# Compression and rotation ahead of the delta rule's matrices, in tiles of their own, with half-array products in pairs

## The chip, the core and the metric

The kernel runs on one core of one Trainium2 chip. The metric is the device time of one execution in microseconds. The engines are TensorE (PE, with its weight loads as PEld), VectorE (DVE), ScalarE (ACT), GpSimd (POOL) and SyncE (SP, which here only starts transfers).

## The reference, cut to what matters

A trunk of two layers over 256 tokens of width 1024. Each layer has a mixer with two branches, the gated delta rule (a) and attention (b), mixed by gates, and then a feed-forward part: dense in layer 0, eight experts in layer 1.

```python
for l in range(DEPTH):
    h = rms_norm(x, norm_mix[l]) * (1.0 + sc_m) + sh_m
    proj = h @ w_in[l]
    ...
    o_a = gated_delta_rule(d_q, d_k, d_v, beta, g_log)
    o_a = rms_norm(o_a, dn_norm[l]) * jax.nn.silu(dn_z.reshape(b_, s_, DN_HEADS, DN_DV))
    y_a = o_a.reshape(b_, s_, DN_HEADS * DN_DV) @ w_oa[l]
    n_q = apply_rope(rms_norm(n_q...), cos, sin)             # s_k and w_k likewise
    k_c = compress_blocks(c_k...)                            # then norm and rotation; v_c likewise
    o_b = nsa_core(n_q, k_c, v_c, s_k, s_v, w_k, w_v, gates) # compressed, selected, window
    y_b = o_b @ w_ob[l]
    gate_a, gate_b = jnp.split(jax.nn.sigmoid(m_g), 2, -1)
    x = x + g_m * ((gate_a * y_a + gate_b * y_b) @ w_out[l])
    h = rms_norm(x, norm_ffn[l]) * (1.0 + sc_f) + sh_f
    x = x + g_f * (swiglu(h, ...) if l % 2 == 0 else moe_ffn(h, ...))

# gated_delta_rule, chunks of 64 tokens: lower and a_intra are products over the head's
# 64 dimensions times a decay; tinv is the inverse of a unit lower triangle
lower = where(strict, einsum('nbhcd,nbhsd->nbhcs', kb, kc) * decay, 0)
tinv = triangular_solve(eye + lower, eye)
a_intra = where(tril, einsum('nbhcd,nbhsd->nbhcs', qc, kc) * decay, 0)
# compress_blocks: 15 windows of 32 tokens, 2 groups
blk = x[:, idx] + pos_emb                                    # 32 * 64 numbers a window
return silu(blk @ w1) @ w2
```

## The kernel before

Tokens lie in two tiles of 128. Large products are made in three parts from a high and a low piece of each operand (lines 242 to 244, or 373 to 375 for the tiles called pn). The pieces of a weight are made on ACT (line 236) and DVE (line 238), after SP's queue has brought it into a ring of slots: a slot is free again when DVE has made the low piece.

The order in which the program is written sets priorities, and a scheduler makes from it the fixed order of each engine: an instruction written later may fill a hole if its tiles are free. A tile with a tag takes its place in turn with the other tiles of that tag, so a later tile waits until the earlier one has had its last reader. PSUM has eight banks: three for "dn" (delta rule), two for "ns" (attention), two for "pj" (projections) and one more.

The mixer (line 435) is written in this order:

1. The projections of the delta rule's inputs (pj), the short convolution and norms, some projections of attention (pn, into npq and npk).
2. The delta rule's matrices. For four heads at a time: the keys times their write strength (kb, line 577), the decays on a pair of masks (pd, lines 588 to 596, exponentials E0 and E1), then for each head the products pS of keys with kb and with the queries (qk). Each pS has 64 dimensions in the contraction, thus half the array's rows. DVE multiplies it with the decay (line 604 for the 512 columns of the first token tile, 609 for the second).
3. The inverse, on blocks of 16: a chain of 15 steps of three DVE instructions (the tile UU, lines 622, 623, 624), which starts at line 618 and ends at line 637. Products of 32 and 64 (py, p, p2, lines 641 to 663) make it whole. Then the recurrence over chunks (pz, pw, pX, po, lines 674 to 696), and the norm of the result (of, to line 722).
4. Attention's compression (lines 726 to 784). Transposed windows (zbk) times the first weights give pcc, one branch (keys, values) after the other with 64 output columns, thus half the array's columns. After the activation (s1, s2) come the second weights (pkv), norm and rotation (kvc, kd), the transposed keys (pkc, kcT) and the values (pvb).
5. The other projections of attention, norm and rotation of queries and keys (rn, npq, npk, qr), and their transposes (pt, into qT and kT).
6. Attention: compressed() (psc), then the window and selected parts in eight groups: scores pSs, masked on DVE to pr, exponentials on ACT, transposes (ppt), products with the values (pob). The tile acc gathers them.
7. The mixing gates (function gates, line 926): 96 products for each 512 columns into pj, and Tanh on ACT (line 931) into a tile mg0 or mg1. Then the branch outputs, and the product with w_out.

In the order that the scheduler makes, much of 4 to 7 is laid between 2 and 3. The constants lie in one tile ct, 1290 columns wide; 406 of these are a pad, and from the masks on the tile is used again for the router's row of gate factors (gfr). The tile E0 shares its tag with qT, L32 with the attention's transposed weights pT, the masks with kT, and zbk with qs.

Layer 1's experts (function moe) take their weights from the same queue (line 1181). They begin at 915 us in the profiled execution.

Of the kernel before, what the change touches and what calls it, by code (L numbers as in the profile page):

```python
# [16 lines left out]
P = 128  # L17
# [23 lines left out]
def const_table():  # L41
# [34 lines left out]
    parts["pad"] = np.zeros((P, 406), np.float32)  # L76
# [11 lines left out]
def trunk(ctx, tc, A, out, dbg=None, stop=None):  # L88
# [39 lines left out]
    def bc(ap, shape):  # L128
        return ap.to_broadcast(shape)
# [257 lines left out]
    cs = cst.tile([P, 2, 3, 32], F32, name="cs")  # L387

# [46 lines left out]
    def mixer(l, hx, mp, late, begun=()):  # L435
# [87 lines left out]

        pq = bank("dn", "pq")
# [30 lines left out]
        masks = mq.tile([P, 2, P], F32R, tag="kT", name=f"masks{l}")  # L555
# [9 lines left out]
        L32 = T([P, 16, 32], "L32", 2, tag="pT")  # L565
# [3 lines left out]
        for hh, hs in enumerate(halves):  # L569
# [9 lines left out]
            E0 = T([P, 4, NT, P], "E0", tag="qT")  # L579
# [18 lines left out]
            for a in range(4):  # L598
                h_ = hh * 4 + a
                b, r = h_ // 2, slice((h_ % 2) * 64, (h_ % 2) * 64 + 64)  # L600
                pS = bank("dn", "pS")
                mm(pS[:, 0:S], kf[r, b, 0:P], kb[r, b], start=True, stop=True)
                mm(pS[:, S:2 * S], kf[r, b, 0:P], qf[r, b], start=True, stop=True)
                V.tensor_tensor(L0[hh][:, a], v2(pS), bc(E0[:, a, None].rearrange("p o t i -> p o (t i)"), [P, 2, S]),
                                op=OP.mult)
                pS = bank("dn", "pS")
                mm(pS[:, 0:P], kf[r, b, P:S], kb[r, b, P:S], start=True, stop=True)
                mm(pS[:, P:S], kf[r, b, P:S], qf[r, b, P:S], start=True, stop=True)
                V.tensor_tensor(L1[:, h_], v2(pS[:, 0:S]), bc(E1[:, a, None], [P, 2, P]), op=OP.mult)
# [113 lines left out]

        proj(npc, 0, 256)

        s1 = T([64, 2, 32], "s1")
        s2 = T([64, 2, 32], "s2")
        w2 = T([64, 2, 64], "w2c")
        nc.scalar.dma_start(w2, A["w_cmp2"][l].rearrange("k d e -> d k e"))
        for kv in range(2):  # L730
            zb = T([P, 16, 31], "zbk", tag="zb")
            pz = bank("ns", "pzc")
            for g in range(2):
                for t in range(NT):
                    tr(pz[:, g * S + t * P:g * S + t * P + P], npc[:, t, kv * 2 + g].rearrange("p a d -> p (a d)"))
# [864 lines left out]
```

## Time and profile before

| | |
|---|---|
| median of three runs | 1817.03 us (1811.85 to 1820.92) |
| the profiled execution | 1813.39 us, of which the span is 1811.6 us |
| mean granted clock of PE | 0.961 of full speed |

The page shows the busy time of each engine, the chain of work that ended last, and the costliest groups of instructions. A row of the timeline has the start in us, the length in us, the engine, the line, the operation, the tile written and the tiles read, the shape, and how many instructions it stands for; in square brackets is the idle time of the engine ahead of it, and what ended that. Matmuls are pipelined, so the step from one start to the next, not the length, says what one costs. A row of a group has the busy time, the mean length of one in ns, and the idle time ahead of them with what ended most of it.

### The profile page before, as it was taken

How to read it: one execution, taken by the hardware profiler on the slowest of the kernel's cores; microseconds unless marked ns; L12 is line 12 of the kernel's file. 1: busy time of each engine (PE TensorE's matmuls, PEld its weight loads, DVE VectorE, ACT ScalarE, POOL GpSimd, SP SyncE). 2: the span in 40 equal slices, each digit the busy share in tenths (PEclk: the TensorE clock that was granted, in tenths of full speed). 3: DMA queues.
4: the chain of work that ended last, by engine and by line, in shares of the span. 5: the costliest groups of instructions: out<-in, count | busy, mean ns of one | idle time of the engine just before them, and what ended most of it. 6: DMA issues, size and time to landing. Idle time of an engine off the chain costs nothing.

```text
span 1811.6 us, 29467 instructions
## 1 busy us (share of the span) xinstructions
PE 1736.5 (96%) x11324; PEld 1386.8 (77%) x11324; DVE 1271.8 (70%) x2146; ACT 935.2 (52%) x1372; POOL 61.4 (3%) x114
## 2 busy tenths in 40 slices
PE   6889799899999999999999999999999999999997
PEld 4879678899999898987888735788885367878732
DVE  6769757799995777834699713888984078999811
ACT  3664344444444574543477602777772067777600
POOL 4300000100000100000100000000000000000000
PEclk8899779999999899988999999999999999999999
DMA  9547325599984334413779999999999999999997
GB/s 336 162 141 255 119 72 190 205 345 329 329 278 151 125 111 135 157 47 140 266 271 367 328 397 404 409 403 409 377 363 360 403 409 407 405 399 362 345 392 277
DMA packets 206362, 515.38 MB, mean 284 GB/s; under 512 B 18862, under 2 KB 58358, under 8 KB 206214
## 3 DMA queue, kind: packets, MB, share of 16 engines
q1 hardware_dynamic: 196806, 509.45, 75.9%
q10 hardware_dynamic: 9312, 3.90, 0.8%
q8 instruction: 91, 1.49, 0.3%
q14 instruction: 57, 0.47, 0.1%
q0 software_dynamic: 96, 0.07, 0.0%
HBM read 512.34 MB, written 1.05 MB: 283 GB/s over the span
## 4 chain that ended last, share of the span: by engine, by line
PE 90%; DVE 5%; ACT 2%; issue 1%; DMA 1%; ACTq 0%; DVEq 0%
PE ph L1204 21%; PE py L1235 11%; PE ph L1267 8%; PE pj L242 8%; PE pj L244 7%; PE pj L243 7%; PE py L1294 4%; PE pSs L876 2%; PE pob L896 2%; PE py L244 2%; PE py L242 1%; PE py L243 1%; PE pn L373 1%; PE pn L375 1%; PE pn L374 1%
## 5 line engine op out<-in xcount | busy, mean ns | idle before, releaser
L238 DVE TENSOR_TENSOR wml<-m,wmh 128x1024 fp32r<-128x1024 f32 (+1 forms) x300 | 311.1, 1078 | 34.3 <-ACT wmh L236 31.4
L236 ACT ACTIVATE wmh<-m 128x1024 fp32r<-128x1024 f32 (+1 forms) x302 | 276.5, 945 | 64.1 <-PE ph L1204 36.8
L1204 PE MATMUL ph<-wml,gh 128*128 128x512 f32 x560 | 181.7, 397 | 2.0 <-DVE wml L238 2.0
L1204 PE MATMUL ph<-wmh,gl 128*128 128x512 f32 x560 | 181.9, 394 | 0.0
L1204 PE MATMUL ph<-wmh,gh 128*128 128x512 f32 x560 | 181.6, 394 | 0.2 <-ACT gh L1144 0.2
L236 ACT ACTIVATE w2h<-m 128x1024 fp32r<-128x1024 f32 x130 | 134.7, 1057 | 41.8 <-PE py L1235 28.3
L238 DVE TENSOR_TENSOR w2l<-m,w2h 128x1024 fp32r<-128x1024 f32 x130 | 152.6, 1220 | 5.1 <-ACT w2h L236 4.8
L1235 PE MATMUL py<-w2h,uu 128*128 128x512 f32 x560 | 152.8, 394 | 0.0
L1267 PE MATMUL ph<-m,gs 128*64 128x512 f32 (+1 forms) x720 | 139.7, 537 | 0.0
L1204 PEld LDWEIGHTS ph<-wml,gh 128*128 128x128 f32 x560 | 103.8, 188 | 32.1 <-DVE wml L238 7.3
L242 PE MATMUL pj<-hf0h,wh 128*128 128x256 f32 x448 | 127.1, 285 | 1.2 <-ACT hf0h L344 1.2
L243 PE MATMUL pj<-hf0l,wh 128*128 128x256 f32 x448 | 126.7, 284 | 0.0
L244 PE MATMUL pj<-hf0h,wl 128*128 128x256 f32 x448 | 126.5, 285 | 0.0
L1204 PEld LDWEIGHTS ph<-wmh,gh 128*128 128x128 f32 x560 | 105.0, 188 | 26.3 <-ACT wmh L236 1.6
L1235 PEld LDWEIGHTS py<-w2h,uu 128*128 128x128 f32 x560 | 105.1, 188 | 24.5
L1204 PEld LDWEIGHTS ph<-wmh,gl 128*128 128x128 f32 x560 | 105.1, 188 | 24.2
L263 DVE SCALAR_TENSOR_TENSOR adacc<-ada,cact,adacc 128x512 f32<-128x512 f32 x158 | 117.3, 757 | 2.5 <-DMA ada<-in_w_ada_dram 1.4
L1267 PEld LDWEIGHTS ph<-m,gs 128*64 128x64 f32 x720 | 51.3, 137 | 81.9 <-issue 74.0
L236 ACT ACTIVATE wh<-w 128x1024 fp32r<-128x1024 f32 x56 | 59.4, 1061 | 95.0 <-PE pj L243 60.5
L1277 DVE TENSOR_TENSOR u<-u,ph 128x512 f32<-128x512 f32 (+1 forms) x12 | 7.5, 622 | 135.8 <-PE ph L1267 135.8
L236 ACT ACTIVATE wh<-win 128x1024 fp32r<-128x1024 f32 x64 | 67.3, 1056 | 66.1 <-PE pj L243 48.6
L1235 PE MATMUL py<-w2l,uu 128*128 128x512 f32 x280 | 90.1, 403 | 0.0
(637 smaller groups left out, 3980.6 us busy)
## 6 DMA issues: line engine op xcount, KB each, us to landing
m<-in_w_moe_dram SPq DMA_DIRECT2D x313, 1024.0 KB, 12.2
ada<-in_w_ada_dram SPq DMA_DIRECT2D x48, 1024.0 KB, 7.3
w<-in_w_dense_dram SPq DMA_DIRECT2D x42, 1024.0 KB, 7.4
win<-in_w_in_dram SPq DMA_DIRECT2D x34, 1024.0 KB, 5.1
xT<-in_w_moe_dram SPq DMA_DIRECT2D x23, 1024.0 KB, 11.9
wout<-in_w_out_dram SPq DMA_DIRECT2D x8, 1024.0 KB, 5.0
win<-in_w_in_dram SPq DMA_DIRECT2D x8, 536.0 KB, 3.8
win<-in_w_in_dram SPq DMA_DIRECT2D x8, 528.0 KB, 3.5
```

The costliest lines, as they stand in the source:

```text
L236: SC.activation(hi, src, AF.Copy)
L238: cur["last"] = eng.tensor_tensor(lo, src, hi.bitcast(F32), op=OP.subtract).ins
L242: mm(o, w[0], x[0], start=start, stop=False, skip_group_check=True)
L243: mm(o, w[0], x[1], start=False, stop=False, skip_group_check=True)
L244: mm(o, w[1], x[0], start=False, stop=stop, skip_group_check=True)
L263: V.scalar_tensor_tensor(acc, w(k), cact[:, k:k + 1], acc, op0=OP.mult, op1=OP.add)
L876: mm(pS[:, i * 2 * nk:(i + 1) * 2 * nk], qT[r, b0 + i, t * P:(t + 1) * P], kT[r, :, 0:nk], start=True, stop=True)
L896: mm(po[:, c0:c0 + 64], pT[:, (2 * i + j) * (t + 1) + kt], npk[:, kt, o + g * 64:o + g * 64 + 64], start=(b0 + i + j + kt == 0), stop=(b0 ...
L1204: mm(p_, s_[:, k], d_[:, i * 512:i * 512 + 512], start=k == 0 and d_ is hi and s_ is gh, stop=k == KT - 1 and d_ is lo)
L1235: mm(p_, s_[:, j], d_[:, n * 512:n * 512 + 512], start=q + j == 0 and d_ is hi and s_ is uh, stop=q == 3 and j == nb - 1 and d_ is lo)
L1267: mm(p_[i * 64:i * 64 + 64, 0:h], self.g[:, k], raw[:, i * h:i * h + h], start=k == 0, stop=k == KT - 1, skip_group_check=True)
L1294: mm(self.py[n * 64:n * 64 + 64], self.u[q][:, b, i * 64:i * 64 + 64], raw[:, n * 512:n * 512 + 512], start=q + j == 0, stop=q == 3 and j ...
```

## The change

1. The blocks 4 and 5 above (all of attention's projections, compression, norm, rotation) are written ahead of block 2.
2. E0 and L32 become parts of a new tile eb, which has the tag of mg0, the first gate tile; the masks have a tag of their own; zbk takes the tag mt in two places. So no tile of the matrices is shared with attention; eb is shared with the gates instead.
3. pcc of the two branches goes to the two column halves of one bank, the products in turn; s1, s2 and the second weights have 128 partitions, the branches in the two halves, and pkv has two banks.
4. pS of two heads, in the two row halves, is written in turn into two banks.
5. The pad of the constants is dropped. gfr's second half lies in the tile vb; the router's lg and before move from vb to cs.

```diff
-    parts["pad"] = np.zeros((P, 406), np.float32)
...
-    lg = vb[:, 0, 0:24].rearrange("p (t e) -> p t e", e=8)
-    before = vb[:, 0, 24:88].rearrange("p (e o) -> p e o", e=8)
...
+    csf = cs.rearrange("p a t n -> p (a t n)")
+    lg = csf[:, 0:24].rearrange("p (t e) -> p t e", e=8)
+    before = csf[:, 24:88].rearrange("p (e o) -> p e o", e=8)
+    gfr = (ct[:, COFF["los"][0]:COFF["los"][0] + 512], vb.rearrange("p l n -> p (l n)")[:, 0:512])
...
+        proj(npc, 0, 256)
+        s1 = T([P, 32], "s1c")
+        s2 = T([P, 32], "s2c")
+        w2 = T([P, 64], "w2c")
+        nc.scalar.dma_start(w2, A["w_cmp2"][l].rearrange("k d e -> (k d) e"))
...
+            zb = T([P, 16, 31], "zbk", 2, tag="mt")
...
+            for a in range(8):
+                for kv in range(2):
+                    mm(pc[kv * 64:kv * 64 + 64, 0:31], w1s[kv][:, a * 64:a * 64 + 64], zbs[kv][:, a8 * 8 + a],
+                       start=a8 + a == 0, stop=a8 * 8 + a == 15)
...
+        pkv = [bank("ns", "pkv") for _ in range(2)]
+        for kv in range(2):
+            r = slice(kv * 64, kv * 64 + 64)
+            mm(pkv[kv][0:30, 0:64], s1[r, 0:30], w2[r], start=True, stop=True)
...
         pq = bank("dn", "pq")
...
-        masks = mq.tile([P, 2, P], F32R, tag="kT", name=f"masks{l}")
+        masks = mq.tile([P, 2, P], F32R, tag="masks", name=f"masks{l}")
+        eb = T([P, 2048], "eb", tag="mg0")
...
-        L32 = T([P, 16, 32], "L32", 2, tag="pT")
+        L32 = eb[:, 1024:1536].rearrange("p (n i) -> p n i", n=16)
...
-            E0 = T([P, 4, NT, P], "E0", tag="qT")
+            E0 = eb[:, 0:1024].rearrange("p (h t i) -> p h t i", h=4, t=NT)
...
-            for a in range(4):
-                h_ = hh * 4 + a
-                b, r = h_ // 2, slice((h_ % 2) * 64, (h_ % 2) * 64 + 64)
-                pS = bank("dn", "pS")
-                mm(pS[:, 0:S], kf[r, b, 0:P], kb[r, b], start=True, stop=True)
-                mm(pS[:, S:2 * S], kf[r, b, 0:P], qf[r, b], start=True, stop=True)
...
+            for a in range(0, 4, 2):
+                b = hh * 2 + a // 2
+                rs = [slice(0, 64), slice(64, 128)]
+                pS = [bank("dn", "pS") for _ in rs]
+                for o, src in ((0, kb), (S, qf)):
+                    for p_, r in zip(pS, rs):
+                        mm(p_[:, o:o + S], kf[r, b, 0:P], src[r, b], start=True, stop=True)
...
-        proj(npc, 0, 256)
...
-                for a in range(8):
-                    mm(pc[0:64, 0:31], w1[:, a * 64:a * 64 + 64], zb[:, a8 * 8 + a], start=a8 + a == 0, stop=a8 * 8 + a == 15)
...
-        proj(npb, 264, 264)
-        proj(npk, 0, 268)
-        proj(npk, 268, 268)
```

The lines that moved without a change are left out. In the changed file the lines have other numbers: pS is made in lines 723 and 730, the chain of the inverse is lines 741 to 747, the projections are lines 239 to 241.

The first place is PE's order in layer 0, at the matrices. Before, the products pS of one head stand between the three-part products pn of attention's projections:

```order
L373 MATMUL pn<-wnh,hm0h 128x268
L374 MATMUL pn<-wnl,hm0h 128x268
L375 MATMUL pn<-wnh,hm0l 128x268
L602 MATMUL pS<-kb_934,qk_580 128x256
L603 MATMUL pS<-qk_580 128x256
L373 MATMUL pn<-wnh,hm0h 128x268
L374 MATMUL pn<-wnl,hm0h 128x268
L375 MATMUL pn<-wnh,hm0l 128x268
L607 MATMUL pS<-kb_934,qk_580 128x128
L608 MATMUL pS<-qk_580 128x128
```

In the changed kernel all pn stand ahead, and between the matrices stand the ends of compression (pkc, pvb) and rotation (pt):

```order
L125 MATMUL pc<-ct,cx_1485 128x128 x4
L125 MATMUL pkc<-ct,kd_1034 128x30
L595 MATMUL pvb<-kvc_1010,ct 128x512
L706 MATMUL pd<-ge_1392,masks_1395 128x512 x4
L712 MATMUL pd<-gs_1393,masks_1395 128x512 x2
L714 MATMUL pd<-ge_1392,masks_1395 128x512 x2
L723 MATMUL pS<-kb_1391,qk_580 128x256
L723 MATMUL pS<-qk_580 128x256
L125 MATMUL pt<-ct,qr_1271 128x128 x4
L125 MATMUL pt<-ct,npk_478 128x128 x2
```

No projection is left among them; 96 gate products stand ahead of this piece, and the next ones after the first groups of attention.

The second place is DVE's order in layer 0, in the chain of the inverse (UU). Before, the rows of the rotation (rn0y, npk), of the compression's norm (rc0y), of the modulation (modc) and weight splits (wl) stand between the steps:

```order
L622 STREAM_SHUFFLE UU_945<-UU_945 128x16x3
L147 SCALAR_TENSOR_TENSOR rn0y<-rn0u,rn0y 128x24
L144 SCALAR_TENSOR_TENSOR rc0y<-rc0u,rc0y 30x1
L288 TENSOR_TENSOR modc_106<-pada,cols 128x4
L238 TENSOR_TENSOR wl<-win_1536_2613,wh 128x1024
L623 TENSOR_TENSOR UU_945<-UU_945 128x16x3
L149 TENSOR_SCALAR rn0y<-rn0y 128x24
L145 TENSOR_TENSOR rc0u<-rc0y 30x1
L238 TENSOR_TENSOR wl<-win_1536_2611,wh 128x1024
L624 TENSOR_TENSOR UU_945<-UU_945 128x16x3
```

In the changed kernel three steps follow with nothing between but one row of the attention's softmax (sm):

```order
L745 STREAM_SHUFFLE UU_1403<-UU_1403 128x16x2
L919 TENSOR_TENSOR sm_1999<-sm_1999,sg_511 128x8
L746 TENSOR_TENSOR UU_1403<-UU_1403 128x16x2
L747 TENSOR_TENSOR UU_1403<-UU_1403 128x16x2
L745 STREAM_SHUFFLE UU_1403<-UU_1403 128x16x3
L746 TENSOR_TENSOR UU_1403<-UU_1403 128x16x3
L747 TENSOR_TENSOR UU_1403<-UU_1403 128x16x3
L745 STREAM_SHUFFLE UU_1403<-UU_1403 128x16x4
L746 TENSOR_TENSOR UU_1403<-UU_1403 128x16x4
L747 TENSOR_TENSOR UU_1403<-UU_1403 128x16x4
```

The rows of rotation and compression that stood there now come ahead of the chain.

The third place is PE's order in layer 1, toward the end of attention. Before, the groups of attention stand together, with transposes (ppt, pc) and without projections:

```order
L896 MATMUL pob<-npk_6662,pT_8566 128x64 x4
L876 MATMUL pSs<-kT_8284,qT_8283 128x512
L126 MATMUL ppt<-ct,pr_8574 128x128 x2
L126 MATMUL pc<-ct,cx_7859 128x128 x4
L896 MATMUL pob<-npk_6662,pT_8584 128x64 x4
L126 MATMUL ppt<-ct,pr_8592 128x128 x2
L876 MATMUL pSs<-kT_8284,qT_8283 128x512
L126 MATMUL ppt<-ct,pr_8592 128x128 x2
L126 MATMUL pc<-ct,cx_7869 128x128 x4
L896 MATMUL pob<-npk_6662,pT_8602 128x64 x4
```

In the changed kernel the recurrence (pX, po) and gate products (pj, of which hm1h and hm1l are the normed input) lie between the groups:

```order
L914 MATMUL pob<-npk_6655,pT_8570 128x64 x4
L125 MATMUL ppt<-ct,pr_8578 128x128 x4
L894 MATMUL pSs<-kT_7598,qT_7597 128x512
L810 MATMUL pX<-W_8160,TT_7944 64x64 x8
L818 MATMUL po<-L_7729,acc 64x256 x2
L241 MATMUL pj<-hm1h,wl 128x256
L239 MATMUL pj<-hm1h,wh 128x256
L240 MATMUL pj<-hm1l,wh 128x256
L241 MATMUL pj<-hm1h,wl 128x256
L239 MATMUL pj<-hm1h,wh 128x256
L240 MATMUL pj<-hm1l,wh 128x256
L914 MATMUL pob<-npk_6655,pT_8588 128x64 x4
```

The gate products that stood ahead of attention now come in such runs to its end.

More of the change, by code (lines that the diff above doesn't have):

```diff
@@ new lines, in mixer @@
+        pc = bank("ns", "pcc")
+        for a8 in range(2):
+            w1s = []
+            for kv in range(2):
+                w1 = cur["tmp"].tile([P, 512], F32, tag="adacc", name=f"wc1{l}{kv}{a8}", bufs=2)
+                nc.scalar.dma_start(w1.rearrange("p (a e) -> p a e", a=8),
+                                    A["w_cmp1"][l][kv][a8 * 1024:(a8 + 1) * 1024].rearrange("(a p) e -> p a e", p=P))
+                w1s.append(w1)
+            for a in range(8):
+                for kv in range(2):
+                    mm(pc[kv * 64:kv * 64 + 64, 0:31], w1s[kv][:, a * 64:a * 64 + 64], zbs[kv][:, a8 * 8 + a],
+                       start=a8 + a == 0, stop=a8 * 8 + a == 15)
@@ new lines, in mixer @@
+        V.tensor_tensor(kvc[0:30, 0], kvc[0:30, 0], tca[0:30], op=OP.mult)
+        kd = T([32, 2, 64], "kd")
+        for d in range(2):
+            V.tensor_tensor(kd[0:30, d], kvc[0:30, 0], kvc[0:30, 2], op=OP.add)
+        dbg(f"kvc{l}", kvc[0:30]); dbg(f"kd{l}", kd[0:30])
+        kcT = T([P, 32], "kcT")
+        V.memset(kcT, 0.0)
+        pc = bank("ns", "pkc")
+        tr(pc[:, 0:30], kd[0:30].rearrange("p a d -> p (a d)"), 30)
+        for g in range(2):
+            V.tensor_copy(kcT[g * 64:g * 64 + 64, g * 16:g * 16 + 15], pc[g * 64:g * 64 + 64, g * 15:g * 15 + 15])
@@ new lines, in mixer @@
+        cmpb = T([P, 1024], "cmpb", tag="npc")
+        vbk = cmpb[:, 0:512].rearrange("p (h d) -> p h d", h=8)
+        pc = bank("ns", "pvb")
+        mm(pc, C["selv"][0:30], bc(kvc[0:30, 1][:, None, :], [30, 8, 64]), start=True, stop=True)
+        V.tensor_tensor(vbk, v8(pc), bc(C["hblk"][:, :, None], [P, 8, 64]), op=OP.mult)
+        proj(npb, 264, 264)
+        proj(npk, 0, 268)
+        proj(npk, 268, 268)
+        sigm(sg[:, :, 8:32], npk[:, :, K_NG:K_NG + 24])
+        nr = T([P, NT, 12], "nr")
@@ new lines, in mixer @@
+        groups = ((npb, C_Q, 0, 8, 0), (npk, 0, 8, 2, 1), (npk, K_WK, 10, 2, 2))
+        view = lambda tl, t, o, n: tl[:, t, o:o + 64 * n].rearrange("p (h d) -> p h d", d=64)
+        for t in range(NT):
+            qs = T([P, 12, 64], "qs", tag="zb")
+            for tl, o, j, n, _ in groups:
+                SC.activation(qs[:, j:j + n], view(tl, t, o, n), AF.Square)
+            V.tensor_reduce(nr[:, t], qs, axis=AX.X, op=OP.add)
+        rn = rsq(nr.rearrange("p t h -> p (t h)"), 24, 1.0 / 64, f"rn{l}", 1.0).rearrange("p (t h) -> p t h", t=NT)
@@ L756, in mixer @@
-        pc = bank("ns", "pkv")
-        for kv in range(2):
-            mm(pc[0:30, kv * 64:kv * 64 + 64], s1[:, kv, 0:30], w2[:, kv], start=True, stop=True)
-        kvc = T([32, 3, 64], "kvc")
-        kr = T([32, 1], "kr")
-        V.tensor_copy(kvc[0:30, 0:2], pc[0:30, 0:P].rearrange("p (k d) -> p k d", k=2))
-        SC.activation(kvc[0:30, 2], kvc[0:30, 0], AF.Square)
-        V.tensor_reduce(kr[0:30], kvc[0:30, 2], axis=AX.X, op=OP.add)
-        rc = rsq(kr[0:30], 1, 1.0 / 64, f"rc{l}", 1.0)
@@ L967, in mixer @@
         if l:
-            gfr = ct[:, COFF["los"][0]:COFF["los"][0] + D]
             for q in range(2):
@@ L1307, in scatter @@
                     fin(t, n, po[n])
-        gfr = ct[:, COFF["los"][0]:COFF["los"][0] + D]
         gf2 = T([P, 512], "gf2")
```

164 lines of the change are left out of this document (70 added, 94 removed).

## The prediction

> **What bounds the kernel now.** I read the page's totals and chain first, then one table of busy time by stage, then the timeline of PE and of DVE where that table shows a loss.
>
> ```profile
> span 1811.6 us, 29467 instructions
> PE 1736.5 (96%) x11324; PEld 1386.8 (77%) x11324; DVE 1271.8 (70%) x2146; ACT 935.2 (52%) x1372; POOL 61.4 (3%) x114
> PE 90%; DVE 5%; ACT 2%; issue 1%; DMA 1%; ACTq 0%; DVEq 0%
> ```
>
> PE is busy 96% of the span and carries 90% of the chain that ended last. So only three things can shorten the kernel: PE's 75 us of idle time, PE work done at a low granted clock, and PE work removed. The next view is by stage; its columns are the length, the busy time of PE, PEld, DVE, ACT, POOL, the granted clock, the DMA share and GB/s.
>
> ```profile
> 80.00:158.00 78.00, 71.03 (x531) 63.63 (x530) 58.22 (x119) 51.84 (x120) 0.00 (x0) 0.96 0.49 163
> 158.00:217.00 59.00, 48.86 (x349) 43.84 (x347) 52.85 (x183) 22.98 (x49) 0.00 (x0) 0.91 0.55 190
> 217.00:246.00 29.00, 27.18 (x483) 22.67 (x481) 16.55 (x47) 10.82 (x27) 0.00 (x0) 0.53 0.18 59
> ...
> 600.00:706.00 106.00, 101.04 (x746) 93.88 (x747) 74.03 (x171) 67.42 (x147) 8.65 (x35) 0.92 0.37 118
> 706.00:767.00 61.00, 60.07 (x675) 56.40 (x675) 53.21 (x179) 32.22 (x63) 0.00 (x0) 1.00 0.41 140
> 767.00:786.00 19.00, 18.93 (x225) 16.81 (x224) 7.08 (x26) 8.88 (x24) 0.00 (x0) 0.50 0.14 54
> 786.00:826.00 40.00, 39.65 (x343) 31.07 (x343) 15.28 (x46) 19.50 (x46) 0.00 (x0) 0.97 0.31 107
> 826.00:848.00 22.00, 19.80 (x74) 13.02 (x74) 12.40 (x36) 7.07 (x18) 0.00 (x0) 0.63 0.19 67
> ...
> 915.00:1812.00 897.00, 878.75 (x4107) 603.10 (x4106) 603.49 (x706) 494.28 (x577) 0.00 (x0) 1.00 0.98 376
> ```
>
> From 915 us on PE is full at full clock: the change can only shift that part. The losses of the mixers are in five stages. In 158 to 217 PE idles 10.1 us and loses 4.4 to the clock (48.86 x 0.09). In 217 to 246 it idles 1.8 and loses 12.8 (27.18 x 0.47). In layer 1, 767 to 786 loses 9.5 to the clock and 826 to 848 loses 2.2 idle and 7.3 to the clock. The timeline of PE shows what these are.
>
> ```profile
> 188.79 0.31 PE L126 MATMUL pkc<-ct,kd 30*128 30x30 f32 x1 [7.21 <-DVE kd L772]
> ...
> 195.05 0.41 PE L242 MATMUL pj<-hm0h,wh 128*128 128x256 f32 x1
> 195.26 0.41 PE L243 MATMUL pj<-hm0l,wh 128*128 128x256 f32 x1
> ...
> 200.53 0.28 PE L244 MATMUL pj<-hm0h,wl 128*128 128x256 f32 x1
> 200.65 0.28 PE L242 MATMUL pj<-hm0h,wh 128*128 128x256 f32 x1
> ...
> 209.18 1.00 PE L896 MATMUL pob<-npk,pT 128*128 128x64 f32 x8
> 219.66 1.97 PE L896 MATMUL pob<-npk,pT 128*128 128x64 f32 x8
> ```
>
> PE waits 7.21 us at pkc for kd, the end of the compression, whose small DVE steps stand between the steps of the matrices' inverse. Behind that wait one gate product (pj) takes 0.21 us from start to start instead of 0.12. From 217 on attention and the inverse's 32x32 products (py) run with no gate product between them, and the same eight pob products take 1.97 us instead of 1.00.
>
> **What the change removes.** Compression and rotation come ahead of the matrices, so kd is ready before pkc needs it, and the inverse's chain no longer carries their rows. The gate products then lie between attention and the inverse (PE order of the changed kernel), not ahead of them. That such a mixture keeps the clock is seen after the bad stage, where runs of gate products stand between pz, pw, pX, pob and pSs:
>
> ```profile
> 246.00:261.00 15.00, 15.00 (x125) 12.74 (x125) 5.45 (x17) 7.44 (x18) 0.00 (x0) 1.00 0.50 172
> ```
>
> So I take back in layer 0 the 11.9 us of idle time of 158 to 246 and 15 of the 17.2 lost to the clock (the rest for stretches that stay without gate products). In layer 1 I take 9 of 9.5 and 9 of 9.5. The Trainium skill ("TensorE: Matmul & The Clock Gate", Part 1, What's actually happening) says the same in general: the slow clock is the default, and a busy window of about 3.4 us releases it. Its Part 4 says that transposes in transpose mode do not count as busy, which speaks against the gain, since attention is full of ppt; by that, the mixed stages could fall to half clock as a whole. The row above, ppt among its products, shows 1.00, and the sum goes by the row.
>
> **The pairs.** pS is now two heads in the two row halves, pcc both branches in the two column halves.
>
> ```profile
> 693.21 0.70 PE L602 MATMUL pS<-kb,qk 64*128 64x256 f32 x2
> 693.75 0.59 PE L603 MATMUL pS<-qk 64*128 64x256 f32 x2
> 694.27 0.77 PE L749 MATMUL pcc<-zbk,wc 128*64 128x31 f32 x10
> 694.97 0.49 PE L607 MATMUL pS<-kb,qk 64*128 64x128 f32 x2
> 695.29 0.38 PE L608 MATMUL pS<-qk 64*128 64x128 f32 x2
> 695.61 0.30 PE L749 MATMUL pcc<-zbk,wc 128*64 128x31 f32 x2
> ...
> 807.31 1.15 PE L679 MATMUL pz<-acc,TT 64*64 64x64 f32 x32
> 811.59 1.14 PE L683 MATMUL pw<-acc,L 64*64 64x64 f32 x16
> ```
>
> One head costs from start to start 0.54 + 0.52 + 0.32 + 0.32 = 1.70 us, eight heads 13.6. That products in separate parts of the array run together is seen from pz against pw: 32 instructions in pairs take as long as 16 of the same shape alone. Half of 13.6 with a little start-up is 7.6, a gain of 6 a layer. A pcc row takes 0.07 us; 64 a layer are 4.5, the pairs save 2. Together -8 a layer; the bounds are 0 (nothing overlaps) and -9. Against pS stands that its results must be read by DVE:
>
> ```profile
> L609 DVE TENSOR_TENSOR L<-pS,E 128x256 f32<-128x256 f32 x16 | 6.7, 421 | 5.9 <-PE pS L608 5.9
> L604 DVE TENSOR_TENSOR L<-pS,E 128x512 f32<-128x512 f32 x8 | 5.5, 690 | 4.3 <-PE pS L603 3.0 <-ACT E L597 1.3
> L604 DVE TENSOR_TENSOR L0b<-pS,E 128x512 f32<-128x512 f32 x8 | 5.4, 678 | 3.1 <-PE pS L603 2.4 <-ACT s L752 0.7
> ```
>
> These are 8 x 0.68 + 8 x 0.42 = 8.8 us a layer, above 7.6: where PE has nothing else, the pair is worth 13.6 - 8.8 = 4.8. The rows also show DVE waiting for pS, 5.9 + 3.0 + 2.4 = 11.3 us in both layers, so DVE is not yet the limit. The Trainium skill ("TensorEngine Tiling (Array Packing)", PSUM Bottleneck) warns of this: tiling quickens TensorE but not the reading of PSUM. Taken strictly the pS pairs bring nothing, and the gain would be 12 us smaller; the waits in the rows above say otherwise.
>
> **What the change costs.** E0 and L32 now lie in eb, whose place the first Tanh result of the gates needs. So gate products stop after two PSUM banks (96 products) until the inverse's first readers of eb are done. In layer 0 these 96 come before the matrices; from the first kb to the first chain step PE's order holds only pd, pS, pkc, pvb, pt and attention's first pSs, ppt and pob, about 21 us of work: 16 of pd, pS and transposes, 5 of attention. DVE's order for the same piece holds, beside the 8.8, five multiplications of 0.69 (E and kb), six weight splits, eleven accumulations of the modulation (adacc) and the rotation.
>
> ```profile
> L238 DVE TENSOR_TENSOR wl<-win,wh 128x1024 fp32r<-128x1024 f32 x14 | 17.0, 1216 | 1.4 <-ACT wh L236 1.2
> L263 DVE SCALAR_TENSOR_TENSOR adacc<-ada,cact,adacc 128x512 f32<-128x512 f32 x23 | 17.0, 740 | 0.2
> L812 DVE TENSOR_TENSOR npq<-npq,taba 128x512 f32<-128x512 f32 x2 | 1.3, 673 | 0.0
> ```
>
> 6 x 1.22 = 7.3, 11 x 0.74 = 8.1, 3.5 for the five, and an estimated 5 for that part of the rotation that stands after the first kb (four rows of about 0.67, the rest smaller): 33 us. With waits between engines (PE, ACT's exponentials, DVE, in turn) I put 41, so 20 us in which PE has nothing. Bounds: 0, if gate-free work of the other stages fits in, and 31, if the piece lasts as long as the present one without its projections. I take 20, because DVE's sum is counted and only the 8 of waits is guessed. In layer 1 96 gate products lie between the pS: 96 x 0.12 = 11.5 us of cover, so 9.
>
> Where the projections pn end on PE in layer 0, and where the chain of the inverse begins and ends on DVE:
>
> ```profile
> 137.81 0.28 PE L375 MATMUL pn<-wnh,hm0l 128*128 128x268 f32 x1
> ...
> 157.93 0.48 DVE L618 SCALAR_TENSOR_TENSOR UU<-L,ct,UU 128x256 f32<-128x256 f32 x1
> 212.67 0.35 DVE L637 TENSOR_SCALAR TT<-UU,ct 128x256 f32<-128x256 f32 x1
> ...
> 706.47 0.48 DVE L618 SCALAR_TENSOR_TENSOR UU<-L,ct,UU 128x256 f32<-128x256 f32 x1 [0.19 <-ACT UU L617]
> 758.40 0.35 DVE L637 TENSOR_SCALAR TT<-UU,ct 128x256 f32<-128x256 f32 x1
> ```
>
> The chain (L618 to L637) lasts 54.7 and 51.9 us, and it starts later now: in layer 0 at about 172 (the pn end at 137.8; ahead of that six heads of pS, 10.2, and an estimated 5 of pd and transposes go away and an estimated 8 of gate products come in, so the matrices begin at 131, plus 41), in layer 1 at about 724 (an estimate: 96 gate products, 11 us, and 7 of pn and pcc, now stand ahead of it). But its rows stand nearly together in DVE's order, so I take 32 us in layer 0: it ends at 204 against 212.67, and PE, not the chain, sets the end of the mixer.
>
> Edits at nothing: the shorter constant (no transfer is on the chain there), the copies of kvc and w2 (a few rows of 0.2 on DVE, inside the 33), the moves of lg and gfr (same work). On SP's queue the change swaps a few loads: a dense tile ahead of wout in layer 0 and m0 to m2 ahead of wout in layer 1, each with some 20 us or more before its first use. If that cover is gone, the price is one landing, 5 us for wout. ACT's tables are loaded as often as before. The experts after 915 shift one to one, because their loads wait for the computation, not it for them:
>
> ```profile
> SPq L1181 <- DVE wml L238: 282.6, 124, 7.6
> ```
>
> **The sum.** Layer 0: -11.9 - 15 - 8 + 20 = -15 (bounds -30, everything regained at a cost of 5, and +23, nothing regained and 31 lost, less the pairs). Layer 1: -9 - 9 - 8 + 9 = -17 (bounds -29 and 0). Together -32: the profiled execution would take 1813.4 - 32 = 1781; the median of the three runs shown is 3.6 us above it, so 1784 to 1785, and I say **1784**.
>
> **Rivals.** (a) More: DVE's piece overlaps as it does now, new idle time 5 instead of 29: 1784 - 24 = 1760, chance 0.14. For it: PE idles only 7 us in 80 to 158 although DVE does 58 us of work there. Against it: that stage has projections between. (b) No change: the gate-free matrices cost 31 and 20 us instead of 20 and 9, 1806, and with half of the clock loss, 17, kept as well 1823; or the DMA stream of the experts (share 0.98 after 915) does not follow an earlier start and swallows the 32, 1816. Chance 0.13. Against it: SP's waits on wml. (c) Slower: the mixed stages run at half clock. The 250 and 215 gate products between attention and small products then (counted in PE's order) lose 0.21 - 0.12 = 0.09 each, 42 us, against -32: 1784 + 42 = 1826; it decides from 355 products on. What speaks for it is the row 217 to 246, half clock as soon as small products are alone; against it is 246 to 261. Chance 0.06. By Part 4 of the page on TensorE in the Trainium skill it would be this case. (d) Slower: the inverse starts 14 and 18 us later and its chain, 54.7 and 51.9 us, does not become shorter; what follows it is late by 32: 1817 + 32 = 1849; it decides where the chain saves less than its delay. Chance 0.05.
>
> **How the numbers follow.** The forecast holds 0.62, with its own range 1770 to 1800. The range of 8 in 10 takes in (a) down to 1758 and the nearer part of (b) up to 1815. Half a per cent, 9 us, is what a measurement of this kernel can tell from no change; faster than 1808 are the forecast, (a) and a little of (b): 0.77. Same, most of (b): 0.12. Slower, (c) and (d): 0.11.
>
> **What the profile after would show.** The 7.21 us at pkc are gone. A stage before the chain in layer 0 with PE half busy and a low clock, from about 131 to 172. First and last row of the chain at about 172 and 204, then about 724 and less than 45 us more. A clock of about 1.00 where py, pob and ppt stand among gate products. Experts starting at about 883 instead of 915. I am wrong if PE idles more than 30 us in the new stage of layer 0, if the mixed stages show a clock under 0.8, or if the chain of waits moves to DVE.

## The result, and the profile after

The changed kernel takes 1790.88 us (median of 4 runs, 1787.5 to 1793.0) against 1816.82 us for the kernel before (4 runs): a ratio of 0.9857, 95% interval 0.9828 to 0.9886. Run again in a later job (E9) it gave 0.9861 (0.9827 to 0.9895). The forecast of 1784, with its own range 1770 to 1800, had the direction and the size; but the way there was in good part another.

The page of the changed kernel, first and fourth part:

```profile
span 1788.8 us, 29436 instructions
PE 1715.6 (96%) x11324; PEld 1373.2 (77%) x11324; DVE 1263.3 (71%) x2138; ACT 934.4 (52%) x1370; POOL 61.7 (3%) x114
PE 91%; DVE 5%; ACT 2%; DMA 1%; issue 1%; POOL 0%; ACTq 0%; DVEq 0%
```

PE is as full as it was, with the same 11324 products, but busy 21 us less. Where, the timeline's marks tell (first product of a stage, in us):

| stage | before | after | difference |
|---|---|---|---|
| mixer of layer 0 (first pn to the product with w_out) | 28.37 to 322.48 | 28.47 to 317.87 | -4.7 |
| w_out, dense part, norms | to 609.44 | to 602.51 | -2.3 |
| mixer of layer 1 (to the branch output) | to 847.37 | to 824.59 | -15.9 |
| to the first expert product | to 914.00 | to 891.50 | +0.3 |
| experts | to 1811.6 | to 1788.8 | -0.3 |

The trace has the steps of the granted clock, so each stage can be split in three: PE's idle time; the time lost to the clock (PE's busy time in each step, times one minus the granted share); and the remainder, which is what PE's work would have taken at full clock (called work below). In us, before and after:

| stage | idle | lost to the clock | work |
|---|---|---|---|
| mixer of layer 0 | 26.5, 25.1 | 26.8, 29.8 | 240.8, 234.4 |
| mixer of layer 1 | 4.3, 5.3 | 23.8, 11.1 | 209.8, 205.6 |
| whole span | 75.1, 73.2 | 56.3, 47.3 | 1680.2, 1668.4 |

So less than half of the gain is the clock (9.0 us); 11.8 are work that takes less time even at full clock, and 1.9 idle time. In layer 0 more is lost to the clock than before. The changed kernel was profiled once more in E9; its mixers there have 25.1, 29.2 and 234.5 in layer 0, and 6.5, 13.1 and 205.5 in layer 1.

Busy time by stage, first of layer 1 (before, then after; columns as in the prediction):

```profile
700.00:720.00 20.00, 20.00 (x161) 19.29 (x161) 16.95 (x62) 12.92 (x28) 0.00 (x0) 1.00 0.30 106
740.00:840.00 100.00, 98.66 (x1008) 80.70 (x1007) 51.58 (x162) 47.43 (x117) 0.00 (x0) 0.82 0.28 96
```

```profile
700.00:720.00 20.00, 16.69 (x75) 11.23 (x73) 18.59 (x55) 8.05 (x19) 0.00 (x0) 0.75 0.15 53
740.00:840.00 100.00, 98.88 (x1166) 84.98 (x1165) 55.83 (x137) 49.27 (x101) 0.00 (x0) 1.00 0.41 140
```

The inverse, the recurrence and attention ran at a mean clock of 0.82 and now run at 1.00, which is 17.5 us by the steps. A part of it is given back from 700 to 720, among the matrices, where the clock is now 0.75 and PE idles 3.3 us. In layer 0 (after):

```profile
80.00:138.00 58.00, 50.71 (x431) 49.78 (x431) 36.92 (x85) 34.22 (x74) 0.00 (x0) 0.88 0.58 185
138.00:177.00 39.00, 30.08 (x129) 21.01 (x127) 32.75 (x107) 20.91 (x58) 0.00 (x0) 0.74 0.27 93
177.00:215.00 38.00, 38.00 (x280) 35.66 (x280) 35.92 (x126) 17.32 (x41) 0.00 (x0) 0.91 0.41 139
215.00:281.00 66.00, 66.00 (x886) 55.45 (x885) 37.82 (x76) 34.26 (x73) 0.00 (x0) 0.97 0.44 146
281.00:318.00 37.00, 32.32 (x234) 31.13 (x234) 27.21 (x51) 12.43 (x16) 0.00 (x0) 0.86 0.67 234
```

The half clock of 217 to 246 is gone (0.97), but there are two holes: the matrices (8.9 us idle and 8.7 lost to the clock, by the steps) and the end of the mixer (4.7 idle and 4.8 lost). The last stretch of the mixer before the change, which is 4.5 us longer, had 3.3 idle and 1.7 lost:

```profile
281.00:322.50 41.50, 38.22 (x291) 34.44 (x287) 31.61 (x62) 18.14 (x33) 0.00 (x0) 0.96 0.57 204
```

The waits of PE in the two holes, in brackets:

```profile
146.26 0.48 PE L730 MATMUL pS<-kb,qk 64*128 64x128 f32 x2 [2.42 <-ACT eb L715]
...
154.86 1.11 PE L125 MATMUL pc<-ct,cx 128*128 128x128 f32 x4 [2.35 <-DVE L L725]
155.91 0.31 PE L125 MATMUL pkc<-ct,kd 30*128 30x30 f32 x1
...
175.99 1.10 PE L914 MATMUL pob<-npk,pT 128*128 128x64 f32 x8 [2.34 <-ACT pT L909]
...
298.73 0.66 PE L125 MATMUL pc<-ct,cx 128*128 128x128 f32 x4 [1.46 <-DVE cx L840]
301.13 0.79 PE L239 MATMUL pj<-oa,wh 128*128 128x256 f32 x2 [1.74 <-ACT oa L971]
```

pkc waits for nothing now. The waits in the matrices go round ACT, DVE and PE, as priced; those at the end are for the last steps of the delta rule's branch (cx, oa).

### The profile page after: what moved, and what is told of

It reads as the page before. It is cut to its first block, busy times and chain, and to the rows that moved or that the text cites. A ratio compares the mean times of both kernels' runs of the same rounds, so it can differ in the third digit from the quotient of the medians.

```text
span 1788.8 us, 29436 instructions
## 1 busy us (share of the span) xinstructions
PE 1715.6 (96%) x11324; PEld 1373.2 (77%) x11324; DVE 1263.3 (71%) x2138; ACT 934.4 (52%) x1370; POOL 61.7 (3%) x114
## 3 DMA queue, kind: packets, MB, share of 16 engines
HBM read 512.13 MB, written 1.05 MB: 287 GB/s over the span
## 4 chain that ended last, share of the span: by engine, by line
PE 91%; DVE 5%; ACT 2%; DMA 1%; issue 1%; POOL 0%; ACTq 0%; DVEq 0%
PE ph L1221 21%; PE py L1252 11%; PE pj L239 8%; PE ph L1284 8%; PE pj L241 8%; PE pj L240 8%; PE py L1311 4%; PE py L241 2%; PE py L239 1%; PE py L240 1%; PE pSs L894 1%; PE pob L914 1%; PE pg L1154 1%; PE put L125 1%; PE pn L370 1%; PE pn L371 1%
## 5 line engine op out<-in xcount | busy, mean ns | idle before, releaser
L235 DVE TENSOR_TENSOR wl<-win,wh 128x1024 fp32r<-128x1024 f32 x60 | 73.3, 1224 | 29.4 <-ACT wh L233 29.2
```

The costliest lines, as they stand in the source:

```text
L235: cur["last"] = eng.tensor_tensor(lo, src, hi.bitcast(F32), op=OP.subtract).ins
```

## The experiments

In every job the kernel before ran on the same chip; ratios are to it. All times are medians over all executions of five rounds. A kernel's order is read from its program, as ahead of the prediction. Only one execution of each was profiled; where that one is far from the median, the text says so. But each execution has its span and its mean granted clock on record, so two more figures can be had for every kernel: the span times the clock, called unthrottled time here, and what is left of the span, called withheld time. Both stand, as medians, in the table behind E12.

**E1 and E2: the pS pairs.** E1 is the changed kernel with pS head by head, E2 the kernel before with the pairs alone.

```diff
-                for o, src in ((0, kb), (S, qf)):
-                    for p_, r in zip(pS, rs):
-                        mm(p_[:, o:o + S], kf[r, b, 0:P], src[r, b], start=True, stop=True)
...
+                mm(pS[:, 0:S], kf[r, b, 0:P], kb[r, b], start=True, stop=True)
+                mm(pS[:, S:2 * S], kf[r, b, 0:P], qf[r, b], start=True, stop=True)
```

> The changed kernel, but the pS products head by head as before (pcc stays paired). The prediction's term: pS pairs are worth 6 us a layer, so 12 us slower than the changed kernel (about 1803). Rival, from the trace after: PE's order has kb and qk of one head side by side, not the two heads in turn, and PE's time for pS in layer 1 fell only from 12.8 to 11.3 us; then 0 to 4 us slower (1791 to 1795).

> The kernel before with the pS pairs alone, nothing else. The prediction's term: 12 us faster than before (about 1805). Rival (pairs not side by side in the order): 0 to 4 us faster (1813 to 1817).

E2 took 1815.92 us against 1813.86: 1.0007 (0.9988 to 1.0025), no gain. The order shows why: in the scheduler's order kb and qk of one head stand side by side, then those of the next. They are in the same half of the array and run one after the other, as the first pS of the changed kernel do, 0.54 us from start to start:

```profile
141.07 0.70 PE L723 MATMUL pS<-kb,qk 64*128 64x256 f32 x2
141.61 0.59 PE L723 MATMUL pS<-qk 64*128 64x256 f32 x2
```

E1 took 1808.19 us, 0.9965 (0.9939 to 0.999), with single executions from 1796.05 to 1817.64. It is slower than the changed kernel by more than either theory said. At full clock its pS take 0.6 us a layer more than those of the changed kernel (11.0 and 11.2 against 10.4 and 10.6), so it isn't mainly the pairing that is missing. Of the 17 us, 10 are withheld time (72 against 63). The profiled execution doesn't show them: it is one of the three shortest of twelve, 1796.85 us.

**E3: let the gate products into the matrices.**

```diff
-        eb = T([P, 2048], "eb", tag="mg0")
+        mga = T([P, KT, S], "mg0")
-        L32 = eb[:, 1024:1536].rearrange("p (n i) -> p n i", n=16)
+        L32 = T([P, 16, 32], "L32", tag="zb")
-            E0 = eb[:, 0:1024].rearrange("p (h t i) -> p h t i", h=4, t=NT)
+            E0 = mga[:, 4:8].rearrange("p h (t i) -> p h t i", t=NT)
```

> The changed kernel, but E0 lies in the second half of the first gate tile itself and L32 in the tag of qs, so the first 96 gate products more can be read out while the matrices are made. Theory 1 (the stop of the gate products at 96 leaves PE 8.8 us idle and at half clock in the matrices of layer 0): 8 to 14 us faster than the changed kernel (1777 to 1783), the clock of 138 to 177 above 0.9. Rival (the chain of the inverse sets the end of layer 0, the gate products only move): within 3 us of the changed kernel.

It took 1821.59 us, 1.0038 (1.0023 to 1.0053): slower even than before, and both theories fell. Two stages of its layer 0:

```profile
138.00:177.00 39.00, 33.50 (x202) 26.89 (x201) 37.79 (x100) 16.85 (x33) 0.00 (x0) 0.87 0.58 205
...
215.00:281.00 66.00, 61.30 (x709) 47.12 (x709) 28.10 (x81) 24.78 (x58) 0.00 (x0) 0.69 0.19 65
```

The matrices are fuller (33.5 against 30.1 us, clock 0.87 against 0.74), as meant. But from 215 to 281 PE has idle time and a clock of 0.69 instead of 0.97; by then the gate products are used up. The unthrottled time is that of the changed kernel (1729 against 1727 us); the whole loss is withheld time, 91 against 63. So a new theory: the gate products (384 a mixer, 96 more for zf are of the same kind) are a stock, and what counts is how much of it is left for the inverse and the recurrence, whose small products ran at half clock when alone. The hold by eb, which the prediction booked as a cost, is what leaves them there.

**E4: use up the stock first.** The blocks of the gates are written ahead of attention:

```diff
+        mga = gates(0)
+        late(2)
+        mgb = gates(1)
         def compressed():
...
-        mga = gates(0)
...
-        late(2)
-        mgb = gates(1)
```

> The changed kernel, but the two gate blocks are written ahead of attention, so that they come first and attention and the recurrence are left with few gate products at their end. Theory 1 (the gain is the clock: gate products between small ones): 12 to 25 us slower than the changed kernel (1803 to 1816), half clock in attention's last groups of both layers. Rival (the gain is the earlier compression and rotation, whose waits are gone): within 4 us of the changed kernel.

1838.72 us, 1.0129 (1.0103 to 1.0154): about 48 us slower than the changed kernel (2.7% by the ratios), twice as much as expected. Most of it is withheld time, 103 us. The last groups of attention in layer 1 stand without gate products:

```profile
840.00:880.00 40.00, 32.90 (x126) 20.72 (x127) 14.58 (x44) 12.01 (x33) 0.00 (x0) 0.66 0.13 47
```

**E5: the tiles alone.** The kernel before with E0 and L32 in eb.

```diff
+        eb = T([P, 2048], "eb", tag="mg0")
-        L32 = T([P, 16, 32], "L32", 2, tag="pT")
+        L32 = eb[:, 1024:1536].rearrange("p (n i) -> p n i", n=16)
-            E0 = T([P, 4, NT, P], "E0", tag="qT")
+            E0 = eb[:, 0:1024].rearrange("p (h t i) -> p h t i", h=4, t=NT)
```

> The kernel before with the tiles alone: E0 and L32 in eb, which has the tag of the first gate tile; no move, no pairs. In PE's order of layer 0 this lays 67 gate products behind the pkc that waited 7.2 us, and little is changed in the inverse. Theory 2 (gate products are a stock; what counts is whether they stand among attention and the inverse; the tile holds them back only together with the move): 0 to 10 us faster than before (1804 to 1814). Rival (the hold of the gates is by itself the gain): 15 to 25 us faster (1790 to 1799).

1823.39 us, 1.0061 (1.0038 to 1.0084): slower, outside the ranges of both theories. Without the move the order still uses up the stock ahead of py, and only 96 products are left behind it, as before. But the withheld time grew from 71 to 82 us with the same 96, so their number doesn't settle the clock alone. The tiles are no gain by themselves.

**E6: pairs by force.** The products with the queries are issued after both with kb.

```diff
+                last = None
                 for o, src in ((0, kb), (S, qf)):
+                    with tc.issue_after(last) if last else ExitStack():
...
+                    last = k_
```

> The changed kernel with the two heads' pS products forced next to each other (the product with the queries is issued after both products with kb), so that the row halves can work together. If pairs overlap as pz did (32 products in the time of 16), PE's time for pS falls by 3 to 5 us a layer: 4 to 8 us faster than the changed kernel (1783 to 1787). Rival (DVE's reading of pS and the wait for the second bank set the pace of the matrices): within 3 us of it, PE's time for pS less but its idle time more.

1800.35 us, 0.9931 (0.9907 to 0.9955), about 0.7% slower than the changed kernel, so both ranges were missed. At full clock the pS of layer 1 now take 8.0 us (10.6 in the changed kernel, 12.8 before; the prediction priced true pairs at 7.6), and a wait grew. What PE waited for ahead of the smaller pS, in us and times, in the changed kernel (line 730) and in E6 (line 735):

```profile
  ACT eb L715: 2.4, 1
  DVE L L725: 0.8, 1
  DVE L0b L725: 0.5, 1
```

```profile
  DVE L0b L728: 3.6, 2
  ACT eb L715: 2.4, 1
  DVE L L728: 1.0, 1
```

With pairs next to each other PE waits 3.1 us more for DVE's reading into L0b, which is more than the 2.6 us that the closer pairs save. By the Trainium skill ("TensorEngine Tiling (Array Packing)", PSUM Bottleneck) tiling does not quicken that reading; here the trace agrees: DVE takes 0.68 us for a large pS in both kernels. The 10 us are mostly something else: the unthrottled time is no longer than that of the changed kernel (1725 against 1727), the withheld time is (73 against 63), and only 96 gate products are left behind py in layer 0 where the changed kernel has 139. (The profiled execution is the shortest of six, 1795.98 us.) So this run doesn't show that the reading of pS makes true pairs a loss.

**E7: half of the move.** Compression stays ahead; the other projections and the rotation come behind the matrices.

```diff
-        proj(npb, 264, 264)
-        proj(npk, 0, 268)
...
         pq = bank("dn", "pq")
...
+        proj(npb, 264, 264)
+        proj(npk, 0, 268)
...
         V.tensor_copy(U, bc(C["id16"][:, None, :], [P, 16, 16]))
```

> The changed kernel, but only compression is ahead of the matrices; the other projections of attention and the rotation are written behind them, so that pn stands between pS again. Theory 2: PE is full in the matrices of layer 0 (8.8 us less idle and 8.7 us less lost to the clock there), but the gate products used meanwhile are missing at py and p2, which cost 10 to 15 us more: within 8 us of the changed kernel (1783 to 1799). Rival (the hole in the matrices is the loss of layer 0): 10 to 17 us faster (1774 to 1781).

1803.66 us, 0.9945 (0.9926 to 0.9964): slower than the changed kernel by about 0.8%, on the side of the stock theory and a little past its range. Filling the matrices with pn gave nothing back: 108 and 96 gate products were left behind py, where the changed kernel leaves 139 and 236, and the withheld time is 74 against 63. (The profiled execution is the longest of nine, 1815.3 us, so its stages in the table below are some 12 us too long in all.)

**E8: pcc one branch after the other.**

```diff
-            for a in range(8):
-                for kv in range(2):
+            for kv in range(2):
+                for a in range(8):
```

> The changed kernel with pcc one branch after the other again, still in the two column halves. The prediction's term: 2 us a layer, 4 us slower than the changed kernel (1795). The trace after shows PE's time for pcc 4.4 to 3.3 us and 4.8 to 2.6 us in the two layers, so 3 us. Rival: nothing measurable, because the PE time saved was idle time elsewhere.

1801.4 us, 0.992 (0.9889 to 0.995). The edit undoes the pairs: PE's time for pcc rose to 3.9 us in each layer (3.4 and 2.6 in the changed kernel; at full clock 2.4 and 2.6), and sixteen products take 1.05 us, 0.066 each:

```profile
671.32 1.12 PE L558 MATMUL pcc<-zbk,wc 128*64 128x31 f32 x16
672.37 0.39 PE L372 MATMUL pn<-wnh,hm1l 128*128 128x268 f32 x1
```

That is 1.8 us of the 10. The unthrottled time grew by 5 us and the withheld time by 4, so the order elsewhere differs too, and its two layers went apart: layer 0 took 286.2 us with 188 gate products behind py (changed kernel 289.4 with 139), layer 1 took 233.4 with 190 (222.1 with 236). How much of the loss is the order, this run doesn't tell.

**E9: the changed kernel again.**

> The changed kernel once more, as a measure beside the next three on the same chip. If its time is one value, 1787 to 1794. If it has two, as the kernel with single pcc showed (1792 to 1794 and 1801 to 1803), also some executions near 1800, which would say that part of what the other kernels lost is not their edit.

1790.24 us, 0.9861 (0.9827 to 0.9895); single executions 1782.9, 1789.64 to 1792.01, and one of 1799.41, so now and then the changed kernel is near 1800 too. The 10 us by which E6, E7 and E8 are slower are still theirs by the median; the interval of E8 touches that of E9.

**E10, E11, E12: the hold alone, and with the move.** The products of the second gate block and of zf are issued only after the last step of the chain: in the kernel before (E10), the changed kernel (E11), and the half move (E12).

```diff
+        turn = V.tensor_scalar(T32[:, :, 16:32], U, od, None, op0=OP.mult).ins
...
+                    with tc.issue_after(turn) if half else ExitStack():
+                        pg_ = chunk_b(raw, hx, b * P)
...
+            with tc.issue_after(turn):
+                pz = v2(chunk_b(raw, hx, b * P))
```

> The kernel before with one thing added: the products of the second gate block and of zf are issued only after the last step of the inverse's chain, so that 261 instead of 96 gate products stand between the first py and the branch output, in both layers. No move, no other tiles, no pairs. Theory 2 (the gain is where the gate products stand): 15 to 25 us faster than before (1788 to 1798), the clock of the py and p2 stages about 1.0 instead of 0.5. Rival (the gain needs compression and rotation ahead of the matrices): the products are missing ahead of py and PE idles or runs slowly there, within 5 us of before.

E10: 1810.97 us, 0.9975 (0.9956 to 0.9994), 5 us faster than before by the ratio where the stock theory said 15 to 25, and the rival up to 5. In layer 1 the half clock did go in good part:

```profile
740.00:840.00 100.00, 98.35 (x1070) 82.56 (x1070) 53.34 (x157) 48.76 (x120) 0.00 (x0) 0.91 0.31 106
```

That is 9.7 us less lost to the clock in this layer, but 3.4 more idle and 2.6 more work. In layer 0 it moved, it did not go. Two stages there, mostly beside the chain and then behind it:

```profile
177.00:215.00 38.00, 32.34 (x378) 25.15 (x377) 29.51 (x104) 15.09 (x47) 0.00 (x0) 0.63 0.25 84
215.00:281.00 66.00, 66.00 (x610) 54.49 (x610) 31.48 (x86) 29.03 (x66) 0.00 (x0) 0.89 0.37 126
```

The longest wait of PE just ahead of them, from the timeline:

```profile
176.28 0.31 PE L126 MATMUL pkc<-ct,kd 30*128 30x30 f32 x1 [4.47 <-DVE kd L772]
```

pkc still waits, 4.47 us, and from 177 to 195 us attention runs beside the chain without a gate product (E11, below, has 81 in that time), since those not held back came before pkc. So the stock theory is only half of it. Over all executions the hold alone takes 7 us off the withheld time (73 to 66) and nothing off the unthrottled time (1743), where the changed kernel in the same job has 12 and 15 less. That the hold pays only if other work for PE is ready beside the chain, and that the move makes it ready, fits these rows; no run isolates it.

> The changed kernel with the same hold: 253 instead of 139 gate products behind py in layer 0, 251 instead of 236 in layer 1. Theory 2: layer 0 gains 3 to 6 us, layer 1 nothing: 1784 to 1789. Rival (layer 0 is bound by the chain of the delta rule): no change, or up to 5 us slower because the attention beside the chain loses its gate products.

E11: 1791.01 us, 0.9867 (0.9837 to 0.9897), no measurable difference to the changed kernel. In its profiled execution the mixer of layer 0 is 6.9 us shorter (282.5 against 289.4), with a clock of 1.00 from 215 to its end; the other stages gave more than half of that back (layer 1 +1.5, the dense part +1.8), that execution is the shortest of five, and the median shows no gain. Two stages of its layer 0:

```profile
215.00:281.00 66.00, 65.23 (x658) 54.45 (x658) 35.00 (x80) 31.95 (x68) 0.00 (x0) 1.00 0.45 151
281.00:318.00 37.00, 36.18 (x308) 35.89 (x307) 33.84 (x53) 15.73 (x19) 0.00 (x0) 1.00 0.83 282
```

> Compression alone ahead of the matrices (as in the half move), pairs and tiles as changed, and the same hold: pn between pS again, 113 gate products between pS and py, 271 behind py in layer 0 (258 in layer 1). Theory 2: the matrices of layer 0 are filled and the inverse too, 1773 to 1786, faster than the changed kernel. Rival (DVE's rotation rows, again beside the chain, make it 10 us longer): 1788 to 1800.

E12: 1794.9 us, 0.989 (0.9857 to 0.9923), better than E7 without the hold, not better than the changed kernel. The time is in the rival's range, but its mechanism isn't borne out: the chain lasts 29.9 us in layer 0 (164.2 to 194.1), 8 less than in the changed kernel, not 10 more. What PE does wait for in layer 0 is the rotation: 5.8 us for qr, ahead of pt. No version was found that beats the changed kernel.

All of it in one table: gate products (with those of zf) that stand behind the first py in PE's order, and the length of the two mixers in the profiled execution, from the same marks as above; then unthrottled and withheld time, medians of all executions. For the kernel before these two are from three jobs.

| kernel | layer 0: behind py, us | layer 1: behind py, us | unthrottled, us | withheld, us |
|---|---|---|---|---|
| before | 96, 294.1 | 96, 237.9 | 1742 to 1743 | 71 to 73 |
| E2 (pS pairs, no move) | 96, 301.1 | 96, 234.1 | 1744 | 71 |
| E5 (tiles, no move) | 96, 302.5 | 96, 243.7 | 1739 | 82 |
| E10 (hold, no move) | 261, 294.8 | 262, 234.2 | 1743 | 66 |
| E3 (move without the hold) | 96, 304.1 | 96, 237.4 | 1729 | 91 |
| E7 | 108, 296.5 | 96, 238.2 | 1728 | 74 |
| E6 | 96, 291.1 | 222, 223.5 | 1725 | 73 |
| E1 | 119, 290.8 | 203, 225.7 | 1733 | 72 |
| changed | 139, 289.4 | 236, 222.1 | 1727 | 63 |
| changed again (E9) | 139, 288.8 | 236, 225.0 | 1728 | 61 |
| E8 | 188, 286.2 | 190, 233.4 | 1733 | 67 |
| E11 | 253, 282.5 | 251, 223.6 | 1730 | 59 |
| E12 | 271, 284.8 | 258, 226.7 | 1729 | 64 |
| E4 (ahead of attention) | 192, 309.5 | 192, 252.1 | 1735 | 103 |

The table shows two effects. All kernels with compression ahead of the matrices have 1725 to 1735 us of unthrottled time, those without it 1739 to 1744: this part of the gain, some 15 us, doesn't depend on the gate products. All kernels of the first kind also hold the two branches of pcc in column halves, and no run separates these two edits. The withheld time does depend on the gate products: with the move, and with the gates written last, it falls from 91 us with 192 products behind py in the two layers to 59 to 67 with 375 and more. Without the move, or with the gates written ahead of attention, it doesn't follow their number in this way.

## Why the prediction was right, and where it was wrong

**The sum by kinds.** Taken over both mixers, the prediction booked about -31 us of clock, +15 of idle time (-14 for the waits that go, +29 for the new ones) and -16 of work: -32. The profiled executions have -9.6 of clock, -0.4 of idle time and -10.6 of work: -20.6. So the sum came near by luck: a clock gain booked three times too large was set off by idle time that did not come.

**Right.** The stages that were named did get their clock back: -9 and -9 in layer 1 are most of the 17.5 us from 740 to 840. Compression's wait (7.21 us at pkc) is gone. The new stage of layer 0 has about the length that was worked out, 38 us (139 to 177) for 41, and DVE's 32.75 us of busy time in it is the counted 33. The experts shift one to one. The mixture of transposes, small products and gate products keeps the clock (1.00 from 740 to 840); the rule that transposes do not count as busy (the Trainium skill, "TensorE: Matmul & The Clock Gate", Part 4) did not bring the half clock while enough gate products stood among them. E4, with 24 large products among 126 from 840 to 880, ran at 0.66 there; PE also waits 7.1 us in that stretch, and no run has transposes alone.

**The pairs, -8 a layer: they gave at most -3.0 and -4.5.** At full clock, from start to start, pcc went from 4.4 to 2.4 us in layer 0 and from 4.8 to 2.6 in layer 1, as priced:

```profile
676.50 1.12 PE L558 MATMUL pcc<-zbk,wc 128*64 128x31 f32 x30
677.55 0.39 PE L371 MATMUL pn<-wnl,hm1h 128*128 128x268 f32 x1
```

Thirty products in 1.05 us, 0.035 each instead of 0.07. But pS went only from 11.5 to 10.4 us and from 12.8 to 10.6, and a part of that came without the pairs, since E1 has 11.0 and 11.2. The failed step was to take the source's order of pS for PE's order: the rows of the order shown ahead of the prediction have kb and qk side by side, which is one head's pair. E2 measured the pS pairs alone at nothing. E6, which forces them, has 9.7 and 8.0 us for the 7.6 that were priced, so the price of a true pair was about right. The remaining 3 us of work that went are spread over many groups; no run tells their cause.

**Layer 0, -15: it was -4.7.** The idle time came out better than booked: the 11.9 us went, and the matrices cost 8.9 for the 20. The failed step is the clock, -15: it was +3.0. The stages of the kernel before from 158 to 246 lost 16.4 us to it; what corresponds to them, 177 to 281, loses 5.1. But the matrices lose 8.7, which was not booked at all, the projections from 80 on 1.9 more than before, and the end of the mixer 3.1 more (and idles 1.4 more). For that end the rows offer a reason: the chain starts at 176.9 and ends at 214.9, 38 us instead of 32 and not earlier than the 212.67 of before:

```profile
L741 DVE SCALAR_TENSOR_TENSOR UU<-eb,ct,UU x2: 484/486/487, 176.9 to 718.6; 128x256 f32<-128x256 f32 x2
L760 DVE TENSOR_SCALAR TT<-UU,ct x2: 342/344/346, 214.9 to 747.1; 128x256 f32<-128x256 f32 x2
```

So the delta rule's branch is late again, and PE waits 3.2 us for its cx and oa. "PE, not the chain, sets the end of the mixer" failed in layer 0. In E11 the chain ends at 200.5, gate products are left at that place, these waits are gone and the layer is 6.9 us shorter; which of the two does it, the run doesn't separate. In layer 1 the chain took 28.5 us for 51.9, and the step held.

**The sign of the hold.** The stop of the gate products was booked as a cost of 20 and 9. E3 took it away and lost 1.8% against the changed kernel, with the same unthrottled time and 28 us more withheld: the hold was the means. The clock gain and its cost were booked as if they could be had apart; they can't.

**Layer 1, -17: it was -15.9**, of which -12.6 are the clock (booked: about -16), -4.2 work (booked: -8) and +1.0 idle time (booked: about +7). The second profiled execution has -10.7, -4.3 and +2.2. The bound of -29 for this layer doesn't come out of its terms, whose largest sizes, 9.5, 9.5 and 9, make -28.

**The spread of one kernel** is withheld time. The twelve executions of E1 go from 1796 to 1818 us while their clock goes from 0.966 to 0.953, and their unthrottled time stays between 1730 and 1734. In E8 there are two groups (1791.63 and 1793.54; four from 1801.18 to 1803.23), with clocks of 0.967 to 0.969 and 0.961 to 0.963. The two profiled executions of the changed kernel differ in the same way: that of E9 has a step of 3.4 us to half clock from 678.6 that the first hasn't, and its mixer of layer 1 is 2.9 us longer. So the lengths in the table above carry some us of chance, E1's and E7's most.

**Open.** What makes the clock of one program differ between executions, no run tells. The dense part was 2.3 us shorter in the changed kernel (2.3 in E9), and between 0.2 longer and 0.8 shorter in the others, also without a known cause. How the 15 us of unthrottled time divide between the move, pcc and the rest, no run separates; the rows above give pcc at most 4.2 of it.

## What to carry to other kernels

Split a gain into idle time, time lost to the clock and work before giving it a cause; the sum alone can be right by luck. Large products that can run at any time are a stock: count how many an order leaves for the stages of small products, and read the granted clock there, before asking what is idle. Using them up in a hole elsewhere can cost more than the hole (E3); holding them back was worth little without the move (E10). Read the clock of many executions, not of one. Before a pair of half-array products is priced, look in the engine's order whether the two halves stand next to each other, and what reads the result.

## What was not expected of the hardware

In the changed kernel, with 236 gate products behind the first py of layer 1, the clock was 1.00 from 740 to 840 us; before, with 96 behind it, 0.82. A busy PE alone did not bring the clock back: in E3, right after a wait of 4.70 us, PE was busy 24.90 of 25 us with 32x32 products, attention's products and transposes, without a gate product, and the clock stayed at half.

```profile
222.10 1.93 PE L764 MATMUL py<-TT,Y 32*32 32x32 f32 x128 [4.70 <-DVE TT L761]
```

```profile
222.00:247.00 25.00, 24.90 (x432) 16.92 (x432) 7.30 (x28) 11.41 (x28) 0.00 (x0) 0.50 0.09 34
```

The same 128 py took 1.29 us in the changed kernel, where gate products stand near them:

```profile
222.26 1.29 PE L764 MATMUL py<-TT,Y 32*32 32x32 f32 x128
```
